# Token pairs innermost in the one-hots of a PEER layer, their products moved from GpSimd to VectorE, and an eight-token multiply issued one step later

## The chip, the cores and the metric

The kernel runs on one core of one Trainium2 chip, as one launch. The metric is device microseconds of that core, the median of a few runs. The engines are named as the profile names them: PE is TensorE (PEld its weight loads), DVE is VectorE, ACT is ScalarE, POOL is GpSimd, SP is the engine that issues most of the transfers.

## The reference

The reference is a chain of three transformer blocks on 256 tokens of width 1024. The change lies in the last layer of the third block, a PEER layer: each token picks, for each of 8 heads, 16 of 16,384 experts, and adds up their value rows, weighted.

```
va, ia = lax.top_k(sa, PEER_TOPK)
vb, ib = lax.top_k(sb, PEER_TOPK)
...
eidx = jnp.take_along_axis(cidx, pos, axis=-1)
g = jax.nn.softmax(top, axis=-1).astype(ht.dtype)
u = u_tab[eidx]
v = v_tab[eidx]
a = jax.nn.gelu(jnp.einsum('thkd,td->thk', u, ht))
return jnp.einsum('thk,thkd->td', g * a, v)
```

An expert's number is `ia * 128 + ib`. The kernel does not gather rows. It computes gelu(u h) for all 16,384 experts and all tokens, multiplies each by the weight that the token gives the expert (zero for nearly all), and multiplies the result with the whole table v.

## The kernel before

All large products run on PE as three products of `fp32r` parts: each weight tile of 128x1024 is loaded by SP (`raw`), rounded by ACT to `hi` (line 66), and DVE subtracts to get `lo` (line 67; every second one of the first half of the `peer_u` stream goes to POOL instead). PE then multiplies `hi` by the high part of the activations, `lo` by the high part and `hi` by the low part: 24 matmuls of 256 columns for each weight tile. One such tile with its 24 matmuls is called a step here. The class `Stream` keeps two steps of split weights ahead of PE (`ahead` = 2, three buffers each of `hi` and `lo`).

The PEER layer (`peer`, from line 1352) runs in this order. The `wq` product gives queries; `topk` finds for each token and each head the 16 experts, in the background of the first half of the `peer_u` product (64 steps). It leaves, in bf16 and with the (head, choice) pairs on the partitions, `iat` and `ibt` (first and second index, 128 x 256 tokens) and `gt` (the softmax weight as a sum of three bf16 parts). The product leaves gelu(u h) in `G[0]`, for the first indices 0 to 63, as 128 partitions (second index) by 64 (first index) by 256 tokens in f32. The second 64 steps of `peer_u` do the same for first indices 64 to 127 (`G[1]`). Then 128 steps of `peer_v` multiply G, split by ACT and DVE in `parts` (lines 128 and 124, `zh` and `zl`), with the table v.

The weights of the tokens are brought in by the generator `weigh(half)` (line 1499), which runs in the background: each step of a product calls it once, before that step's weights are split, and it then issues one block of four tokens (two blocks where `t0 % 60` is 0, so 64 blocks in 59 steps). `weigh(0)` runs during the second half of `peer_u` and `weigh(1)` during the first 60 steps of `peer_v`. A block consists of

- `onehots` for the block two ahead: on DVE `e` (256 elements: is the iota equal to the token's first index) and `ob` (512 elements: the same with the second index), on POOL `oa` = `e` times the three parts of `gt` (768 elements). Their pool has three buffers of each;
- on PE, 12 matmuls of 64 columns (line 1513): for each of four tokens and each part of the weight, `ob` of the token as the stationary operand and `oa` as the moving one, into a PSUM bank of eight tokens by 64;
- in every second block, the multiply of eight tokens of G by that bank on DVE (lines 1515 and 1516, 512 elements), right behind the matmuls that fill it.

In the four tokens of a block, before, the innermost index of every one-hot is the expert's index, and the operands that repeat (`iat`, `ibt`, `gt`) have an innermost step of 0:

```
at = lambda x, n: x[:, t0:t0 + 4].unsqueeze(2).to_broadcast([128, 4, n])
self.tt(e, it[:, :, 64 * half:64 * half + 64].to_broadcast([128, 4, 64]), at(iat, 64), OP.is_equal)
```

The order of the instructions on each engine is the order in which the program issues them; there is no scheduler. In each queue the order around a block is thus: one-hots of the block two ahead, matmuls of the block, multiply of G, then the split of the weights two steps ahead (`hi` on ACT, `lo` on DVE), then the step's 24 matmuls on PE.

Of the kernel before, what the change touches and what calls it, by code (L numbers as in the profile page):

```python
# [11 lines left out]
BF = mybir.dt.bfloat16  # L12
# [3 lines left out]
OP = mybir.AluOpType  # L16
# [5 lines left out]
S = 256  # L22
# [64 lines left out]
class Kern:  # L87
# [1264 lines left out]
    def peer(self, out):  # L1352
        nc, tc = self.nc, self.tc
        st = self.ctx
        gp = st.enter_context(tc.tile_pool(name="g0", bufs=1))
        ip = st.enter_context(tc.tile_pool(name="pidx", bufs=1))
        op_ = st.enter_context(tc.tile_pool(name="oneh", bufs=3))
        G = [gp.tile([128, 64, S], FT, name="G0"), None]
        iat = ip.tile([128, S], BF, name="iat")
        ibt = ip.tile([128, S], BF, name="ibt")  # L1360
        gt = ip.tile([128, S, 3], BF, name="gt")
        iob = ip.tile([128, 128], BF, name="iob")
        tk = ExitStack()
        kp = tk.enter_context(tc.tile_pool(name="topk", bufs=1))
        keys = kp.tile([128, 16, 128], FT, name="keys")
# [1 line left out]
        iota = kp.tile([128, 128], FT, name="iota")  # L1367
# [42 lines left out]
            nc.vector.max_index(idx[:, 8:16], vals[:, 8:16], src)  # L1410

        def topk():
            nc.vector.tensor_copy(iob, iota)
            yield
            for og in range(4):
                if og == 3:
# [11 lines left out]
            for j in range(2):  # L1428
                vv = va[j].rearrange("p (h s) k -> p h s k", s=2)
                for (a, n, c, m) in (0, 4, 0, 16), (4, 12, 64, 4):  # L1430
                    self.tt(cand[:, :, c:c + n * m].rearrange("p h (a b) -> p h a b", b=m),
                            vv[:, :, 0, a:a + n].unsqueeze(3).to_broadcast([128, 8, n, m]),
                            vv[:, :, 1, :m].unsqueeze(2).to_broadcast([128, 8, n, m]), OP.add)
                yield
                for h in range(8):
                    top16(top[:, h], pos[:, h], cand[:, h])
                    yield
                nc.vector.tensor_copy(xf, ix[j].rearrange("p (h s) k -> p s k h", s=2))
                pv = pos.rearrange("p h k -> p k h")
                lt, r1, r2, r3 = pk  # L1440

                nc.vector.tensor_scalar(lt, pv, 6, None, op0=OP.logical_shift_right)
                nc.vector.tensor_scalar(r1, pv, 4, None, op0=OP.logical_shift_right)
                nc.vector.tensor_scalar(r2, pv, 2, None, op0=OP.logical_shift_right)
                self.tt(r3, r2, r1, OP.subtract)
                nc.vector.scalar_tensor_tensor(dk, r3, -12.0, lt, op0=OP.add, op1=OP.mult)
                for s in range(2):
                    if s == 0:
                        self.tt(pf, r1, dk, OP.add)
                    else:  # L1450
                        nc.vector.tensor_scalar(r1, pv, 3, None, op0=OP.bitwise_and)
                        nc.vector.tensor_scalar(r2, pv, 12, None, op0=OP.bitwise_and)
                        nc.vector.scalar_tensor_tensor(dk, lt, -1.0, r2, op0=OP.add, op1=OP.mult)
                        self.tt(pf, r1, dk, OP.subtract)
                    self.tt(eq, pf.unsqueeze(2).to_broadcast([128, 16, 16, 8]),
                            jc.unsqueeze(1).to_broadcast([128, 16, 16, 8]), OP.is_equal)
                    yield
                    self.tt(eq, eq, xf[:, s].unsqueeze(1).to_broadcast([128, 16, 16, 8]), OP.mult)
                    yield
                    for n in (8, 4, 2):  # L1460
                        self.tt(eq[:, :, :n], eq[:, :, :n], eq[:, :, n:2 * n], OP.add)
                    self.tt(sel[:, s].rearrange("p (h k) -> p k h", k=16), eq[:, :, 0], eq[:, :, 1], OP.add)
                    yield
                sg = sel[:, 2].rearrange("p (h k) -> p h k", k=16)
                self.tt(sg, top, top[:, :, 0:1].to_broadcast([128, 8, 16]), OP.subtract)
                nc.scalar.activation(sg, sg, AF.Exp)
                nc.vector.tensor_reduce(zz, sg, axis=AX.X, op=OP.add)
                nc.vector.reciprocal(zz, zz)
                self.tt(sg, sg, zz.unsqueeze(2).to_broadcast([128, 8, 16]), OP.mult)
                yield  # L1470
                ps = self.bank()
                for i in range(3):
                    nc.tensor.transpose(ps[:, 128 * i:128 * i + 128], sel[:, i], self.ident)
                js = slice(128 * j, 128 * j + 128)
                nc.vector.tensor_copy(iat[:, js], ps[:, 0:128])
                nc.vector.tensor_copy(ibt[:, js], ps[:, 128:256])

                nc.vector.tensor_copy(gr[:, 0], ps[:, 256:384])
                nc.vector.tensor_copy(gt[:, js, 0], gr[:, 0])
                for n in (1, 2):  # L1480
                    self.tt(gr[:, n % 2], gr[:, (n - 1) % 2], gt[:, js, n - 1], OP.subtract)
                    nc.vector.tensor_copy(gt[:, js, n], gr[:, n % 2])
                yield
            next(w0)
            yield

        def onehots(half, t0):
            e = op_.tile([128, 4, 64], BF, name="e")
            oa = op_.tile([128, 4, 3, 64], BF, name="oa")
            ob = op_.tile([128, 4, 128], BF, name="ob")  # L1490
            it = iob.unsqueeze(1)
            at = lambda x, n: x[:, t0:t0 + 4].unsqueeze(2).to_broadcast([128, 4, n])
            self.tt(e, it[:, :, 64 * half:64 * half + 64].to_broadcast([128, 4, 64]), at(iat, 64), OP.is_equal)
            nc.gpsimd.tensor_tensor(oa, e.unsqueeze(2).to_broadcast([128, 4, 3, 64]),  # L1494
                                    gt[:, t0:t0 + 4].unsqueeze(3).to_broadcast([128, 4, 3, 64]), op=OP.mult)
            nc.vector.tensor_tensor(ob, it.to_broadcast([128, 4, 128]), at(ibt, 128), op=OP.is_equal)  # L1496
            return oa, ob

        def weigh(half):

            ahead = [onehots(half, 0), onehots(half, 4)]
            yield
            g = G[half]
            for t0 in range(0, S, 4):
                oa, ob = ahead.pop(0)
                if t0 + 8 < S:
                    ahead.append(onehots(half, t0 + 8))
                if t0 % 8 == 0:
                    ps = self.bank()
                for i in range(4):  # L1510
                    c = 64 * (t0 % 8 + i)
                    for n in range(3):
                        nc.tensor.matmul(ps[:, c:c + 64], ob[:, i], oa[:, i, n], start=n == 0, stop=n == 2)  # L1513
                if t0 % 8:
                    gv = g[:, :, t0 - 4:t0 + 4].rearrange("p a t -> p t a")
                    self.tt(gv, ps.rearrange("p (t a) -> p t a", a=64), gv, OP.mult)
                if t0 % 60:
                    yield

        w0 = weigh(0)  # L1520
        self.gemm("wq", 8, [4] * 4, S, self.z_rhs(S), evac_q)
# [317 lines left out]
```

## Time and profile before

| | |
|---|---|
| three runs | 2462.96, 2474.38 and 2479.35 us; median 2474.38 us |
| profiled execution | 2463.75 us, of which the span from first to last instruction is 2462.0 us |
| busy share of the span | PE 96%, DVE 74%, ACT 46%, POOL 13% |
| mean granted clock of PE | 0.974 |
| chain that ended last, by engine | PE 76%, DVE 15%, issue 3%, ACT 2%, DMA 2%, POOL 1% |
| oa on POOL (line 1494) | 128 instructions, 228.7 us |

The shares are means over a long program; only the last quarter of it holds the change. The rows below therefore come from stretches: 1817 to 2037 us is the second half of `peer_u` with `weigh(0)`, 2037 to 2259 us is `peer_v` with `weigh(1)`, and 2259 to 2455 us is `peer_v` without it. Times in rows are us from the start of the span, or ns where the row's head says so. In a timeline row the number after the start is the duration of the instruction; successive starts on one engine are what an instruction costs there, since the end of one overlaps the start of the next a little.

### The profile page before, as it was taken

What the parts mean: (1) busy time and instruction counts of PE and PEld (TensorE: products, weight loads), DVE (VectorE), ACT (ScalarE), POOL (GpSimd) and SP (SyncE); (2) the same over time, 40 slices, a digit from 0 to 9 for tenths busy, and PEclk for the clock granted to TensorE, in tenths of its full rate; (3) what the DMA queues carried; (4) which work ended last, traced back from release to release, by engine and by line L of the source; (5) the groups of instructions that cost most, each with busy time, mean ns of one, the idle gap of its engine ahead of it and who ended that gap; (6) DMA issues with size and microseconds to landing.
All of it is one profiled execution on the core that took longest, in us unless ns stands there. A gap on an engine that the chain in (4) does not pass through costs nothing.

```text
span 2462.0 us, 48311 instructions
## 1 busy us (share of the span) xinstructions
PE 2364.7 (96%) x20162; PEld 2288.8 (93%) x20162; DVE 1834.0 (74%) x2924; ACT 1134.5 (46%) x1509; POOL 315.8 (13%) x180
## 2 busy tenths in 40 slices
PE   8999999999999999998899988999989999999999
PEld 8999879999999979998899987999989998898999
DVE  7777657777767767777965565577989999998554
ACT  5444545444444445444654444444543333333443
POOL 0000000000000000000000000024445544543000
PEclk9999989999999989999899987999999999999999
DMA  6576514575567414676456642455544444444554
GB/s 220 180 238 219 174 47 152 179 233 186 173 204 264 160 53 155 200 245 206 146 190 199 193 139 69 147 177 178 177 146 155 146 159 142 138 139 157 186 188 146
DMA packets 114951, 418.80 MB, mean 170 GB/s; under 512 B 13086, under 2 KB 14382, under 8 KB 113708
## 3 DMA queue, kind: packets, MB, share of 16 engines
q1 hardware_dynamic: 113356, 406.46, 50.3%
q0 software_dynamic: 1376, 9.26, 1.0%
q8 instruction: 157, 2.57, 0.4%
q14 instruction: 62, 0.51, 0.1%
HBM read 414.62 MB, written 1.05 MB: 169 GB/s over the span
## 4 chain that ended last, share of the span: by engine, by line
PE 76%; DVE 15%; issue 3%; ACT 2%; DMA 2%; POOL 1%; SPq 0%; DVEq 0%; ACTq 0%; POOLq 0%
PE b L186 19%; PE b L191 19%; PE b L187 19%; DVE lo L67 5%; PE b L1577 4%; PE b L1575 4%; PE b L1576 4%; DVE G L124 1%; DVE ob L1496 1%; DMA raw<-in_dn 1%; ACT hi L66 1%; PE b L1513 1%; DVE e L124 1%; DVE ut L124 1%; PE b L225 1%
## 5 line engine op out<-in xcount | busy, mean ns | idle before, releaser
L67 DVE TENSOR_TENSOR lo<-raw,hi 128x1024 fp32r<-128x1024 f32 (+1 forms) x690 | 910.9, 1331 | 442.3 <-ACT hi L66 441.5
L66 ACT ACTIVATE hi<-raw 128x1024 fp32r<-128x1024 f32 x722 | 755.4, 1056 | 852.0 <-PE b L191 418.9
L186 PE MATMUL b<-zh,hi 128*128 128x256 f32 (+1 forms) x3504 | 1000.9, 286 | 11.1 <-ACT hi L66 8.0
L187 PE MATMUL b<-zh,lo 128*128 128x256 f32 (+1 forms) x3504 | 991.6, 283 | 13.0 <-DVE lo L67 8.9
L191 PE MATMUL b<-zl,hi 128*128 128x256 f32 (+1 forms) x3504 | 985.9, 283 | 4.4 <-DVE zl L286 3.9
L186 PEld LDWEIGHTS b<-zh,hi 128*128 128x128 f32 x3504 | 664.1, 190 | 19.4 <-ACT hi L66 8.7
L187 PEld LDWEIGHTS b<-zh,lo 128*128 128x128 f32 x3504 | 665.4, 190 | 15.1 <-DVE lo L67 10.0
L191 PEld LDWEIGHTS b<-zl,hi 128*128 128x128 f32 x3504 | 661.9, 190 | 7.2 <-DVE zl L286 7.2
L1577 PE MATMUL b<-zh,lo 128*128 128x256 f32 x1024 | 292.4, 286 | 2.3 <-DVE lo L67 2.3
L1575 PE MATMUL b<-zh,hi 128*128 128x256 f32 x1024 | 294.6, 288 | 0.0
L1576 PE MATMUL b<-zl,hi 128*128 128x256 f32 x1024 | 289.4, 283 | 0.0
L187 PE MATMUL b<-ah,lo 128*128 128x272 f32 (+1 forms) x960 | 270.7, 283 | 4.4 <-DVE lo L67 4.4
L186 PE MATMUL b<-ah,hi 128*128 128x272 f32 (+1 forms) x960 | 270.4, 282 | 0.4 <-ACT hi L66 0.3
L191 PE MATMUL b<-al,hi 128*128 128x272 f32 (+1 forms) x960 | 268.2, 282 | 0.0
L1494 POOL TENSOR_TENSOR oa<-e,gt 128x768 bf16<-128x768 bf16 x128 | 228.7, 1787 | 225.2 <-DVE e L124 195.3
L1577 PEld LDWEIGHTS b<-zh,lo 128*128 128x128 f32 x1024 | 195.2, 191 | 5.8 <-DVE lo L67 4.1
L1576 PEld LDWEIGHTS b<-zl,hi 128*128 128x128 f32 x1024 | 198.3, 194 | 0.0
L1575 PEld LDWEIGHTS b<-zh,hi 128*128 128x128 f32 x1024 | 195.4, 191 | 0.0
L187 PEld LDWEIGHTS b<-ah,lo 128*128 128x128 f32 x960 | 180.6, 188 | 5.4 <-DVE lo L67 5.4
L186 PEld LDWEIGHTS b<-ah,hi 128*128 128x128 f32 x960 | 180.5, 188 | 1.0 <-ACT hi L66 1.0
L191 PEld LDWEIGHTS b<-al,hi 128*128 128x128 f32 x960 | 179.6, 188 | 0.0
L67 POOL TENSOR_TENSOR lo<-raw,hi 128x1024 fp32r<-128x1024 f32 x32 | 79.6, 2489 | 156.9 <-ACT hi L66 147.2
(380 smaller groups left out, 2390.4 us busy)
## 6 DMA issues: line engine op xcount, KB each, us to landing
raw<-in_gu SPq DMA_DIRECT2D x176, 512.0 KB, 4.3
raw<-in_peer_u SPq DMA_DIRECT2D x128, 512.0 KB, 3.3
raw<-in_peer_v SPq DMA_DIRECT2D x128, 512.0 KB, 3.3
raw<-in_dn SPq DMA_DIRECT2D x88, 512.0 KB, 4.6
raw<-in_w_adaT SPq DMA_DIRECT2D x48, 512.0 KB, 4.5
raw<-in_w_up SPq DMA_DIRECT2D x32, 512.0 KB, 4.3
raw<-in_w_down SPq DMA_DIRECT2D x32, 512.0 KB, 4.3
raw<-in_w_in SPq DMA_DIRECT2D x30, 512.0 KB, 4.1
```

The costliest lines, as they stand in the source:

```text
L66: nc.scalar.activation(hi[:, :width], raw, AF.Copy)
L67: (nc.gpsimd if gp else nc.vector).tensor_tensor(lo[:, :width], raw, hi[:, :width].bitcast(FT), op=OP.subtract)
L124: self.nc.vector.tensor_tensor(out, a, b, op=op)
L186: nc.tensor.matmul(outs[o], hi[:, w], xh, start=first, stop=False, skip_group_check=True)
L187: nc.tensor.matmul(outs[o], lo[:, w], xh, start=False, stop=False, skip_group_check=True)
L191: nc.tensor.matmul(out, a, b, start=False, stop=kt == KT - 1, skip_group_check=True)
L225: self.nc.tensor.matmul(ss[:, j:j + 1], sq[:, c:c + 128], self.ones[:, 0:1], start=first and j == 0, stop=last, skip_group_check=True)
L1494: nc.gpsimd.tensor_tensor(oa, e.unsqueeze(2).to_broadcast([128, 4, 3, 64]), gt[:, t0:t0 + 4].unsqueeze(3).to_broadcast([128, 4, 3, 64]), o ...
L1496: nc.vector.tensor_tensor(ob, it.to_broadcast([128, 4, 128]), at(ibt, 128), op=OP.is_equal)
L1575: nc.tensor.matmul(dst, hi[:, w], ah[:, a], start=first, stop=False, skip_group_check=True)
L1576: nc.tensor.matmul(dst, hi[:, w], al[:, a], start=False, stop=False, skip_group_check=True)
L1577: nc.tensor.matmul(dst, lo[:, w], ah[:, a], start=False, stop=last, skip_group_check=True)
```

## The change

The innermost two elements of every one-hot are now two tokens. The four tokens of a block are two pairs; `iob` holds each number twice side by side, and `gt` holds each of its three parts contiguously over the tokens. The products `oa` are three DVE instructions of 256 elements, one for each part, in place of one POOL instruction of 768. On PE the operands of a token are then every second element, for the stationary and the moving operand both. The multiply of G walks eight tokens innermost in G, and is issued at the start of the block after the pair of blocks that filled its bank, behind that block's one-hots.

```
-        gt = ip.tile([128, S, 3], BF, name="gt")
-        iob = ip.tile([128, 128], BF, name="iob")
+        gt = ip.tile([128, 3, S], BF, name="gt")
+        iob = ip.tile([128, 128, 2], BF, name="iob")
...
-            nc.vector.tensor_copy(iob, iota)
+            nc.vector.tensor_copy(iob, iota.unsqueeze(2).to_broadcast([128, 128, 2]))
...
         def onehots(half, t0):
-            e = op_.tile([128, 4, 64], BF, name="e")
-            oa = op_.tile([128, 4, 3, 64], BF, name="oa")
-            ob = op_.tile([128, 4, 128], BF, name="ob")
...
-            self.tt(e, it[:, :, 64 * half:64 * half + 64].to_broadcast([128, 4, 64]), at(iat, 64), OP.is_equal)
-            nc.gpsimd.tensor_tensor(oa, e.unsqueeze(2).to_broadcast([128, 4, 3, 64]),
-                                    gt[:, t0:t0 + 4].unsqueeze(3).to_broadcast([128, 4, 3, 64]), op=OP.mult)
-            nc.vector.tensor_tensor(ob, it.to_broadcast([128, 4, 128]), at(ibt, 128), op=OP.is_equal)
+            e = op_.tile([128, 2, 64, 2], BF, name="e")
+            oa = op_.tile([128, 3, 2, 64, 2], BF, name="oa")
+            ob = op_.tile([128, 2, 128, 2], BF, name="ob")
+            pr = lambda x: x[:, t0:t0 + 4].rearrange("p (q t) -> p q t", t=2)
+            wide = lambda x, n: x.unsqueeze(2).to_broadcast([128, 2, n, 2])
+            two = lambda x: x.unsqueeze(1).to_broadcast([128, 2, x.shape[1], 2])
+            self.tt(e, two(iob[:, 64 * half:64 * half + 64]), wide(pr(iat), 64), OP.is_equal)
+            for n in range(3):
+                self.tt(oa[:, n], e, wide(pr(gt[:, n]), 64), OP.mult)
+            self.tt(ob, two(iob), wide(pr(ibt), 128), OP.is_equal)
             return oa, ob
...
+            def times():
+                ps, t0 = done
+                gv = g[:, :, t0:t0 + 8]
+                self.tt(gv, ps.rearrange("p (t a) -> p a t", a=64), gv, OP.mult)
...
                 if t0 % 8 == 0:
+                    if done is not None:
+                        times()
                     ps = self.bank()
...
-                        nc.tensor.matmul(ps[:, c:c + 64], ob[:, i], oa[:, i, n], start=n == 0, stop=n == 2)
+                        nc.tensor.matmul(ps[:, c:c + 64], ob[:, i // 2, :, i % 2], oa[:, n, i // 2, :, i % 2], start=n == 0, stop=n == 2)
                 if t0 % 8:
-                    gv = g[:, :, t0 - 4:t0 + 4].rearrange("p a t -> p t a")
-                    self.tt(gv, ps.rearrange("p (t a) -> p t a", a=64), gv, OP.mult)
+                    done = ps, t0 - 4
                 if t0 % 60:
                     yield
+            times()
+            yield
```

On DVE, two blocks of `weigh(0)` with the splits `lo` of the weights between them stand in the kernel before like this:

```order
L1496 TENSOR_TENSOR ob<-iob,ibt 128x512
L124 TENSOR_TENSOR G_17694<-b,G_17694 128x8x64
L67 TENSOR_TENSOR lo<-raw,hi 128x1024
L124 TENSOR_TENSOR e<-iob,iat 128x256
L1496 TENSOR_TENSOR ob<-iob,ibt 128x512
L67 TENSOR_TENSOR lo<-raw,hi 128x1024
L124 TENSOR_TENSOR e<-iob,iat 128x256
L1496 TENSOR_TENSOR ob<-iob,ibt 128x512
L124 TENSOR_TENSOR G_17694<-b,G_17694 128x8x64
L67 TENSOR_TENSOR lo<-raw,hi 128x1024
```

And in the changed kernel, on DVE at the same place:

```order
L124 TENSOR_TENSOR G_17694<-b,G_17694 128x64x8
L67 TENSOR_TENSOR lo<-raw,hi 128x1024
L124 TENSOR_TENSOR e<-iob,iat 128x256
L124 TENSOR_TENSOR oa<-e,gt 128x256 x3
L124 TENSOR_TENSOR ob<-iob,ibt 128x512
L67 TENSOR_TENSOR lo<-raw,hi 128x1024
L124 TENSOR_TENSOR e<-iob,iat 128x256
L124 TENSOR_TENSOR oa<-e,gt 128x256 x3
L124 TENSOR_TENSOR ob<-iob,ibt 128x512
L124 TENSOR_TENSOR G_17694<-b,G_17694 128x64x8
```

Each block has three instructions `oa` more on DVE, between `e` and `ob`; the multiply of G still comes once in two blocks, with the loops over tokens and indices exchanged.

On POOL, the last rows of the kernel before, with the splits of the first half of `peer_u` and the products `oa`:

```order
L67 TENSOR_TENSOR lo<-raw,hi 128x1024 x30
L1494 TENSOR_TENSOR oa<-e,gt 128x768 x2
L67 TENSOR_TENSOR lo<-raw,hi 128x1024 x2
L1494 TENSOR_TENSOR oa<-e,gt 128x768 x126
```

On POOL in the changed kernel, at the same place:

```order
L67 TENSOR_TENSOR lo<-raw,hi 128x1024 x32
```

POOL has nothing left to do behind the first half of `peer_u`; before, two products `oa` stood ahead of its last two splits.

## Rows read from the trace of the kernel before

**Rows 1.** Busy time by stretch: `weigh(0)`, `weigh(1)`, and `peer_v` alone.
```profile
core 0: us, PE busy (x) PEld busy (x) DVE busy (x) ACT busy (x) POOL busy (x), PEclk, DMA share, GB/s
1817.00:2037.00 220.00, 212.58 (x2296) 209.06 (x2293) 214.39 (x223) 86.08 (x97) 114.17 (x64) 0.98 0.46 152
2037.00:2259.00 222.00, 204.13 (x2166) 197.40 (x2165) 222.00 (x230) 76.63 (x75) 110.70 (x62) 0.97 0.43 139
2259.00:2455.00 196.00, 196.00 (x1668) 196.00 (x1666) 103.11 (x87) 86.93 (x84) 0.00 (x0) 1.00 0.55 177
```
**Rows 2.** Timeline of DVE in `weigh(1)`: start us, duration us, line, out<-in.
```profile
2101.71 0.41 DVE L124 TENSOR_TENSOR e<-iob,iat 128x256 bf16<-128x256 bf16 x1
2102.05 0.68 DVE L1496 TENSOR_TENSOR ob<-iob,ibt 128x512 bf16<-128x512 bf16 x1
2102.65 2.49 DVE L67 TENSOR_TENSOR lo<-raw,hi 128x1024 fp32r<-128x1024 f32 x1
2105.06 0.41 DVE L124 TENSOR_TENSOR e<-iob,iat 128x256 bf16<-128x256 bf16 x1
...
2106.00 1.34 DVE L124 TENSOR_TENSOR G<-b,G 128x512 f32<-128x512 f32 x1
2107.23 1.26 DVE L67 TENSOR_TENSOR lo<-raw,hi 128x1024 fp32r<-128x1024 f32 x1
2108.41 1.21 DVE L124 TENSOR_TENSOR zl<-G,zh 128x1024 fp32r<-128x1024 f32 x1
2109.55 0.41 DVE L124 TENSOR_TENSOR e<-iob,iat 128x256 bf16<-128x256 bf16 x1
```
**Rows 3.** Timeline of POOL at the same place.
```profile
2102.27 1.79 POOL L1494 TENSOR_TENSOR oa<-e,gt 128x768 bf16<-128x768 bf16 x1 [1.56 <-DVE e L124]
```
**Rows 4.** Timeline of PE at the start of `weigh(1)`, where nothing was late.
```profile
2044.72 0.52 PE L1513 MATMUL b<-oa,ob 128*128 128x64 bf16 x12
2045.08 0.36 PE L1575 MATMUL b<-zh,hi 128*128 128x256 f32 x1
...
2048.00 0.52 PE L1513 MATMUL b<-oa,ob 128*128 128x64 bf16 x12
```
**Rows 5.** Tile G, its multiply on DVE: duration ns min/median/max, first and last start us.
```profile
L124 DVE TENSOR_TENSOR G<-b,G x64: 1235/1337/1364, 1819.5 to 2259.3; 128x512 f32<-128x512 f32 x64
```
**Rows 6.** Timeline of DVE in topk: two dependent bf16 instructions, then one that waits for neither.
```profile
1735.13 1.23 DVE L124 TENSOR_TENSOR ce<-pf,jc 128x2048 bf16<-128x2048 bf16 x1
1736.39 1.23 DVE L124 TENSOR_TENSOR ce<-ce,xf 128x2048 bf16<-128x2048 bf16 x1
1737.53 1.22 DVE L67 TENSOR_TENSOR lo<-raw,hi 128x1024 fp32r<-128x1024 f32 x1
```
**Rows 7.** Groups by form on DVE, columns busy us, mean ns of one, idle before.
```profile
L124 DVE TENSOR_TENSOR ce<-ce 128x256 bf16<-128x256 bf16 x4 | 1.2, 292 | 0.1
L124 DVE TENSOR_TENSOR ce<-ce 128x512 bf16<-128x512 bf16 x4 | 1.7, 426 | 0.1
L124 DVE TENSOR_TENSOR t<-b,r 128x512 f32<-128x512 f32 x11 | 7.5, 683 | 0.0
L124 DVE TENSOR_TENSOR gr<-gr,gt 128x128 f32<-128x128 f32 x4 | 1.2, 292 | 0.1
```
**Rows 8.** Tile sel, written at a step of 64 bytes: ns min/median/max.
```profile
L124 DVE TENSOR_TENSOR sel<-ce x4: 372/388/2471, 1730.6 to 1791.2; 128x128 f32<-128x128 bf16 x4
```
**Rows 9.** Weight loads of a one-hot and of an f32 tile: ns min/median/max.
```profile
L1513 PEld LDWEIGHTS <-ob x1536: 95/98/133, 1816.7 to 2258.8; 128*128 128x128 bf16 x192
L1577 PEld LDWEIGHTS b<-zh,lo x552: 187/188/188, 2260.2 to 2454.8; 128*128 128x128 f32 x184
```
**Rows 10.** Timelines of POOL and PE at the end of the first half of `peer_u`.
```profile
1799.47 1.85 POOL L1494 TENSOR_TENSOR oa<-e,gt 128x768 bf16<-128x768 bf16 x1 [2.91 <-DVE e L124]
...
1803.49 5.65 POOL L67 TENSOR_TENSOR lo<-raw,hi 128x1024 fp32r<-128x1024 f32 x2
...
1806.87 0.38 PE L187 MATMUL b<-zh,lo 128*128 128x256 f32 x1 [4.09 <-POOL lo L67]
```

More of the change, by code (lines that the diff above doesn't have):

```diff
@@ L1478, in topk @@
                 nc.vector.tensor_copy(gr[:, 0], ps[:, 256:384])
-                nc.vector.tensor_copy(gt[:, js, 0], gr[:, 0])
+                nc.vector.tensor_copy(gt[:, 0, js], gr[:, 0])
                 for n in (1, 2):
-                    self.tt(gr[:, n % 2], gr[:, (n - 1) % 2], gt[:, js, n - 1], OP.subtract)
-                    nc.vector.tensor_copy(gt[:, js, n], gr[:, n % 2])
+                    self.tt(gr[:, n % 2], gr[:, (n - 1) % 2], gt[:, n - 1, js], OP.subtract)
+                    nc.vector.tensor_copy(gt[:, n, js], gr[:, n % 2])
                 yield
@@ L1487, in onehots @@
         def onehots(half, t0):
-            e = op_.tile([128, 4, 64], BF, name="e")
-            oa = op_.tile([128, 4, 3, 64], BF, name="oa")
-            ob = op_.tile([128, 4, 128], BF, name="ob")
-            it = iob.unsqueeze(1)
-            at = lambda x, n: x[:, t0:t0 + 4].unsqueeze(2).to_broadcast([128, 4, n])
-            self.tt(e, it[:, :, 64 * half:64 * half + 64].to_broadcast([128, 4, 64]), at(iat, 64), OP.is_equal)
-            nc.gpsimd.tensor_tensor(oa, e.unsqueeze(2).to_broadcast([128, 4, 3, 64]),
-                                    gt[:, t0:t0 + 4].unsqueeze(3).to_broadcast([128, 4, 3, 64]), op=OP.mult)
-            nc.vector.tensor_tensor(ob, it.to_broadcast([128, 4, 128]), at(ibt, 128), op=OP.is_equal)
+            e = op_.tile([128, 2, 64, 2], BF, name="e")
[8 more added lines that the diff above has]
+            self.tt(ob, two(iob), wide(pr(ibt), 128), OP.is_equal)
             return oa, ob
@@ L1503, in weigh @@
             g = G[half]
+            done = None
+            def times():
+                ps, t0 = done
+                gv = g[:, :, t0:t0 + 8]
+                self.tt(gv, ps.rearrange("p (t a) -> p a t", a=64), gv, OP.mult)
             for t0 in range(0, S, 4):
```

## The prediction

> **What bounds the kernel now.** I read the stretches first, since the shares of the whole program say only that PE leads. In `peer_v` alone PE is busy for all of 196.00 us, DVE for 103.11 [rows 1]: PE sets the pace, with 1668 matmuls, so 24 of them (a step) take 196 / 1668 x 24 = 2.82 us. Under `weigh(1)` it is the other way round: DVE is busy for all of 222 us, PE for 204.13; under `weigh(0)` DVE has 214.39 of 220 us and PE 212.58 [rows 1]. What the change touches is there the bound.
>
> The timeline of DVE shows how its time goes [rows 2]. By successive starts `e` costs 0.34 us, `ob` 0.60, the multiply of G 1.23, `lo` 1.18, `zl` 1.14. But the other `lo` of each two blocks costs 2.41: it starts at 2102.65, and `oa` runs on POOL from 2102.27 to 2104.06 [rows 3]. It ends 1.08 us after `oa` does, little less than it needs alone: it stood still while POOL ran. The `lo` behind G starts when POOL is done and pays nothing.
>
> These prices rebuild the stretches. `weigh(0)` has 64 `e`, 64 `ob`, 32 G and 63 `lo` (together the 223 instructions of [rows 1]): 64 x 0.94 + 32 x 1.24 + 63 x (1.18 + 2.41) / 2 = 213 us, against 214.39. `weigh(1)` has 62, 62, 32, 60 and 14 `zl` (230): 58 + 40 + 108 + 16 = 222 us, against 222.
>
> PE's floor: 12 matmuls of a block and the 24 of its step take 2048.00 - 2044.72 = 3.28 us where nothing was late [rows 4], 0.46 more than 2.82; the group itself ends after 0.36. I take 0.42 us for a block. `weigh(0)` holds 2296 - 768 = 1528 wide matmuls, 63.7 steps: 63.7 x 2.82 + 64 x 0.42 = 206 us. `weigh(1)` holds 1398, 58.3 steps: 164 + 27 = 191 us.
>
> **The change part by part.** *oa leaves POOL.* 128 instructions go. POOL's own time bounds nothing, but with them goes the standing still of every second `lo`: 1.23 us x 31 in each stretch, 38 us of DVE each. `e` no longer waits for POOL either.
>
> *oa on DVE, e and ob in the new layout.* No row has an innermost run of two. The lower bound is two elements a cycle, as the bf16 instructions of topk show, which also read an operand again and again in their middle dimension: 2048 elements in 1.23 us, 512 in 426 ns, 256 in 292 ns [rows 6, 7]. The upper bound is today's rate, 256 in 410 ns and 512 in 680 ns [rows 2]. Where an instruction needs the result of the one before, the start comes 0.03 us behind the end (1735.13 + 1.23 to 1736.39), where not, some 0.08 us ahead of it (1736.39 + 1.23 to 1737.53) [rows 6]. So at two a cycle a block costs e 0.32, three oa of 0.21, ob 0.35: 1.30 us; at one a cycle 0.44 + 3 x 0.34 + 0.60 = 2.06. I take 1.30, since the rows of topk have the same operations and type and an operand that repeats.
>
> [...]
>
> *Multiply of G.* Now both the read and the write of G step by 1 KB at each element: 1337 ns [rows 5], against 683 for 512 elements out of PSUM with plain steps [rows 7]. `sel`, with only its write at a step, takes 388 ns for 128 elements against 292 [rows 7, 8], 0.75 ns for each. After the change G runs in eights, and the PSUM bank is read at a step of 256 bytes, which no row shows. Bounds: 683 ns (the step costs nothing) and 1337 (nothing gained, as the one stream costs what two did). I take one stream's price, half of 654 ns, and round down: 0.75 us by starts, from 0.60 to 1.24.
>
> *Order of the multiply.* It goes behind the one-hots of the next block. Those already wait for PE to be done with the buffers of the block before, so it adds no wait; the bank is held a step longer. Behind it in DVE's queue stands `lo`, which PE needs two steps later, so 6 us hide it. The closing multiply of `weigh(1)` comes in its own step, two steps ahead of the first split of `G[1]`. The casts of topk: nothing.
>
> *PE.* Count and order stay. The moving operand steps by 4 bytes; f32 operands do so today and pass 256 columns in 0.117 us. The stationary one: below two bounds. At best nothing changes: 12 loads and matmuls of a block in 0.36 us, 0.03 each. At worst a load of a stepped bf16 tile goes as an f32 one, 188 ns against 98 [rows 9], and as dense as those run today, 0.117 us for each pair: 12 x (0.117 - 0.03) = 1.05 us a block. I take nothing, since the number of weights and the type stay.
>
> *End of the first half of `peer_u`.* Two `oa` stand ahead of POOL's last two splits, and PE waits 4.09 us for a split there [rows 10]. Without them the first split starts up to 5 us earlier, against about 2 us of new one-hots on DVE, on which nobody waits soon. Between 1 and 6 us gained; I take 4.
>
> *The sum.* DVE in `weigh(0)`: 64 x 1.30 + 32 x 0.75 + 63 x 1.18 = 182 us, below PE's 206: PE becomes the bound, 220 to 206, 14 us less. `weigh(1)`: 62 x 1.30 + 24 + 60 x 1.18 + 16 = 191 us, level with PE's 191. Two level engines with G and `zl` at uneven places lose something in spite of the two steps between them; I add 4: 195 against 222, 27 us less. With 4 at the start: 45 us less than 2463.75, **2419 us** on the profiled execution's own terms. The three runs have their median 10.6 us above that execution, and scatter from 2463 to 2479; I add half: **2424 us**. The case's own range: G at 1.24 makes `weigh(1)` 207 us for DVE and takes 12 us away; G at 0.60 and the start at 6 give some 5 more. With the runs' scatter 2405 to 2442.
>
> **Rivals.** *A, a pair of tokens is one word, and repeating it costs.* `iat`, `ibt` and `gt` are read as the same 4-byte word 64 or 128 times, a step at every word. If a step costs what it does in `sel`, 0.75 ns a word [rows 7, 8], then 4 x 128 + 256 words add 0.58 us to a block: DVE 219 us in `weigh(0)` and 227 in `weigh(1)`. That is -1, +5 and -4: no change, 2464 (2469 as a median). For it: every stepped stream of this trace is slow. Against: `e` reads one element 64 times today at full rate, topk eight elements 16 times. [...]
>
> *B, no pairs at all.* The layout then only moves `oa` to DVE: a block at 2.06, 0.76 more, 49 us in `weigh(0)` and 47 in `weigh(1)`: 231 and 238, +11 +16 -3, 2488 own, 2493 as a median. Against it are topk's rows.
>
> *C, PE slows, the other side.* If the stepped weight tiles load like f32, a block costs PE 0.42 + 1.05: 274 us in `weigh(0)` and 258 in `weigh(1)`, +54 +36 -4, 2550. The point from which it decides: 45 us over 128 blocks, 0.35 us a block, 0.03 us a load; beyond that the kernel is slower. For it: the bf16 tile's load is half the f32 one's, which says that packing matters; against: a load hides behind its neighbour's 64 columns as far as the group's 0.36 us shows.
>
> [...] No row here has a strided tile.
>
> **How the numbers follow.** Forecast 0.66, A 0.13, B 0.09, C 0.08, something else near no change 0.04. A measurement of this kernel tells about 1%, 25 us, from no change. The forecast lies 45 us down, and with a dear G and a small start still some 30; a tenth of it falls within 1%. Faster 0.60, same 0.26 (A, the rest, a tenth of the forecast, a third of B), slower 0.14 (C and the rest of B). The range goes from 2405 to 2478: it takes in the forecast and A, leaves out C and B.
>
> **What would show it.** `oa` near 292 ns and `ob` near 426 on DVE: the pairs run; 375 and 600 would be A, 410 and 680 B. No `lo` at 2.49 in `weigh`. G between 0.68 and 1.05 us. The group of line 1513 (1526 after) at 0.52 us still; 1.5 is C. PE busy over 98% of both stretches, DVE near 83% in `weigh(0)` and under 100% in `weigh(1)`, and POOL's 4.09 us wait gone. If all durations come as said and the stretches stay over 215 us, the bound was not DVE, and my reading of the first group is wrong.

## The result and the profile after

| | before | after |
|---|---|---|
| median | 2468.67 us (4 runs, 2456.08 to 2479.35) | 2400.73 us (4 runs, 2398.26 to 2405.79) |
| profiled execution | 2463.75 us | 2399.61 us (span 2397.8) |
| mean granted clock of PE | 0.974 | 0.983 |

The ratio is 0.973, with a 95% interval of 0.968 to 0.978: faster, by 64 us between the two profiled executions where the prediction said 45. The median lies 4 us below the range that was stated (2405 to 2478).

The page of the kernel after, its busy shares and the chain that ended last, shows where the time stands now:

```profile
PE 2325.5 (97%) x20162; PEld 2256.3 (94%) x20162; DVE 1752.0 (73%) x3308; ACT 1135.2 (47%) x1509; POOL 87.8 (4%) x52
...
PE 85%; DVE 9%; ACT 2%; DMA 2%; issue 2%; SPq 0%; DVEq 0%; ACTq 0%
```

PE's share of the chain rose from 76 to 85%, DVE's fell from 15 to 9%, and POOL is gone from it.

To compare stretches, both traces are cut at the same three instructions: the first matmul of a block, the first matmul of `peer_v`, and the last matmul of a block; the last stretch ends with the start of the last `peer_v` matmul. The columns are those of [rows 1]. First the kernel before, then the one after:

```profile
1816.70:2038.10 221.40, 213.98 (x2331) 210.41 (x2329) 215.79 (x225) 86.76 (x99) 114.30 (x64) 0.98 0.46 151
2038.10:2258.90 220.80, 202.93 (x2142) 196.25 (x2138) 220.80 (x229) 75.99 (x75) 110.70 (x62) 0.97 0.43 140
2258.90:2456.50 197.60, 197.60 (x1684) 197.60 (x1681) 104.71 (x90) 87.03 (x84) 0.00 (x0) 1.00 0.54 176
```

```profile
1808.40:2014.20 205.80, 205.80 (x2330) 203.64 (x2329) 176.52 (x419) 86.78 (x99) 0.00 (x0) 1.00 0.49 167
2014.20:2202.10 187.90, 187.90 (x2143) 185.79 (x2140) 178.69 (x413) 76.10 (x75) 0.00 (x0) 1.00 0.49 164
2202.10:2392.30 190.20, 190.20 (x1685) 190.20 (x1682) 103.62 (x89) 87.17 (x84) 0.00 (x0) 1.00 0.54 180
```

PE is now busy for the whole of every stretch. `weigh(0)` is 15.6 us shorter, `weigh(1)` 32.9, `peer_v` alone 7.4, although no edit touches it, and what lies ahead of the first of them 8.3: together the 64. The second profiles of the two kernels, further down, are 53 us apart: 56 in the same three stretches, and 3 the other way ahead of them. So the 8.3 us are in part luck; the gains in the three stretches are not.

On DVE the instructions of a block, by tile (ns min/median/max), answer to [rows 5] and to the durations of [rows 2]:

```profile
L124 DVE TENSOR_TENSOR e<-iob,iat x127: 282/286/293, 1800.1 to 2196.2; 128x256 bf16<-128x256 bf16 x127
L124 DVE TENSOR_TENSOR oa<-e,gt x384: 283/287/294, 1799.2 to 2197.0; 128x256 bf16<-128x256 bf16 x192
L124 DVE TENSOR_TENSOR ob<-iob,ibt x128: 416/421/426, 1799.8 to 2197.2; 128x512 bf16<-128x512 bf16 x128
L124 DVE TENSOR_TENSOR G<-b,G x64: 683/686/692, 1813.2 to 2204.1; 128x512 f32<-128x512 f32 x64
L67 DVE TENSOR_TENSOR lo<-raw,hi x125: 1215/1223/1623, 1801.4 to 2199.6; 128x1024 fp32r<-128x1024 f32 x125
```

`e` and `oa` take 286 ns, `ob` 421: topk's durations for 256 and 512 elements of bf16 [rows 7]. No `lo` reaches 2.49 us any more (the longest is 1.62). The timeline of DVE in `weigh(1)` gives the price of a block by starts:

```profile
2101.08 0.29 DVE L124 TENSOR_TENSOR e<-iob,iat 128x256 bf16<-128x256 bf16 x1
2101.48 0.69 DVE L124 TENSOR_TENSOR oa<-e,gt 128x256 bf16<-128x256 bf16 x3
2102.09 0.42 DVE L124 TENSOR_TENSOR ob<-iob,ibt 128x512 bf16<-128x512 bf16 x1
2102.42 1.22 DVE L67 TENSOR_TENSOR lo<-raw,hi 128x1024 fp32r<-128x1024 f32 x1
2103.56 0.29 DVE L124 TENSOR_TENSOR e<-iob,iat 128x256 bf16<-128x256 bf16 x1
...
2104.90 0.69 DVE L124 TENSOR_TENSOR G<-b,G 128x512 f32<-128x512 f32 x1
2105.50 0.28 DVE L124 TENSOR_TENSOR e<-iob,iat 128x256 bf16<-128x256 bf16 x1
```

From `e` to `lo` it is 1.34 us (`e` 0.40, three `oa` 0.61, `ob` 0.33); `lo` costs 1.14, and G 0.60. On PE a block stands like this, to be read against [rows 4]; the tile's weight loads are below it:

```profile
2100.99 0.54 PE L1526 MATMUL b<-oa,ob 128*128 128x64 bf16 x12
2101.36 0.36 PE L1589 MATMUL b<-zh,hi 128*128 128x256 f32 x1
2101.57 0.28 PE L1590 MATMUL b<-zl,hi 128*128 128x256 f32 x1
```

```profile
L1526 PEld LDWEIGHTS <-ob x1536: 96/98/101, 1808.4 to 2202.1; 128*128 128x128 bf16 x192
```

The next product starts 0.37 us behind the block's first matmul, before it was 0.36 [rows 4]; a load takes 98 ns as in [rows 9]. Operands at a step of two elements cost PE nothing that can be seen. The first wide matmul behind a block is 0.20 us ahead of the next one, in both kernels, where the others are some 0.115 apart; with that a block costs PE 0.46 us.

### The profile page after: what moved, and what is told of

Read it like the earlier page. It is cut to its first block, busy times and chain, and to the rows that moved or that the text cites. A ratio compares the mean times of both kernels' runs of the same rounds, so it can differ in the third digit from the quotient of the medians.

```text
span 2397.8 us, 48499 instructions
## 1 busy us (share of the span) xinstructions
PE 2325.5 (97%) x20162; PEld 2256.3 (94%) x20162; DVE 1752.0 (73%) x3308; ACT 1135.2 (47%) x1509; POOL 87.8 (4%) x52
## 4 chain that ended last, share of the span: by engine, by line
PE 85%; DVE 9%; ACT 2%; DMA 2%; issue 2%; SPq 0%; DVEq 0%; ACTq 0%
PE b L186 21%; PE b L191 21%; PE b L187 21%; PE b L1589 5%; PE b L1590 5%; PE b L1591 5%; DVE lo L67 2%; PE b L1526 2%; DMA raw<-in_dn 1%; ACT hi L66 1%; DVE ut L124 1%; DVE ce L124 1%; PE b L225 1%; PE b L508 1%; DVE zl L286 1%
## 5 line engine op out<-in xcount | busy, mean ns | idle before, releaser
L67 DVE TENSOR_TENSOR lo<-raw,hi 128x1024 fp32r<-128x1024 f32 (+1 forms) x690 | 836.6, 1223 | 452.1 <-ACT hi L66 450.1
L191 PEld LDWEIGHTS b<-zl,hi 128*128 128x128 f32 x3504 | 657.8, 189 | 7.6 <-DVE zl L286 7.6
L1589 PE MATMUL b<-zh,hi 128*128 128x256 f32 x1024 | 288.4, 282 | 0.0
L1590 PE MATMUL b<-zl,hi 128*128 128x256 f32 x1024 | 283.2, 277 | 0.0
L1591 PE MATMUL b<-zh,lo 128*128 128x256 f32 x1024 | 283.0, 276 | 0.0
L1590 PEld LDWEIGHTS b<-zl,hi 128*128 128x128 f32 x1024 | 192.6, 188 | 0.0
L124 DVE TENSOR_TENSOR oa<-e,gt 128x256 bf16<-128x256 bf16 x384 | 89.2, 288 | 13.0
```

The lines of the kernel that those rows point to most:

```text
L67: (nc.gpsimd if gp else nc.vector).tensor_tensor(lo[:, :width], raw, hi[:, :width].bitcast(FT), op=OP.subtract)
L124: self.nc.vector.tensor_tensor(out, a, b, op=op)
L191: nc.tensor.matmul(out, a, b, start=False, stop=kt == KT - 1, skip_group_check=True)
L1589: nc.tensor.matmul(dst, hi[:, w], ah[:, a], start=first, stop=False, skip_group_check=True)
L1590: nc.tensor.matmul(dst, hi[:, w], al[:, a], start=False, stop=False, skip_group_check=True)
L1591: nc.tensor.matmul(dst, lo[:, w], ah[:, a], start=False, stop=last, skip_group_check=True)
```

## The experiments

The theory: in `weigh` DVE was the bound, most of all because `lo` stood still while POOL ran; with `oa` in pairs on DVE this goes, and PE becomes the bound. Rivals: a part of the change would do it alone (moving `oa`, or the walk of G), or the order of the multiply matters. Pairs alone, with `oa` on POOL and G strided, were not run. What was open at first sight is why the stretch behind `weigh(1)`, which no edit touches, became 7.4 us shorter. The stages of all runs, by the cuts above, in us; each ratio stands against the runs of the kernel before that were taken along with it. Bumps are extra matmuls, explained below:

| run | `weigh(0)` | `weigh(1)` | `peer_v` alone | median | ratio, 95% interval |
|---|---|---|---|---|---|
| before | 221.4 | 220.8 | 197.6 | 2468.67 | |
| after | 205.8 | 187.9 | 190.2 | 2400.73 | 0.973, 0.968 to 0.978 |
| oa on POOL | 206.8 | 198.1 | 190.2 | 2419.77 | 0.983, 0.980 to 0.986 |
| old layout, oa on DVE | 241.5 | 240.5 | 190.8 | 2497.98 | 1.013, 1.009 to 1.016 |
| before, G in eights | 221.3 | 220.9 | 197.6 | 2463.61 | 1.000, 0.997 to 1.003 |
| after, G strided | 205.8 | 201.0 | 190.2 | 2412.44 | 0.982, 0.976 to 0.987 |
| after, G in its own step | 205.8 | 187.9 | 190.1 | 2408.80 | 0.977, 0.971 to 0.984 |
| 8 matmuls in a block | 202.6 | 184.5 | 197.7 | 2417.62 | 0.978, 0.972 to 0.984 |
| before again | 221.5 | 220.7 | 197.7 | 2469.43 | 1.001, 0.996 to 1.007 |
| before, with bumps | 221.4 | 220.8 | 195.2 | 2462.04 (1 run) | |
| after, with bumps | 205.8 | 187.9 | 194.5 | 2409.87 (1 run) | |
| 9 matmuls | 204.0 | 185.8 | 197.6 | 2407.26 | 0.980, 0.975 to 0.984 |
| 10 matmuls | 206.8 | 188.0 | 197.6 | 2411.80 | 0.980, 0.975 to 0.984 |
| after again | 205.8 | 187.9 | 190.2 | 2407.70 | 0.978, 0.973 to 0.982 |

The stages of one program repeat to 0.2 us. The medians scatter by more, 2400.73 and 2407.70 for the same kernel: in the profiles of these two the first gelu of `G[0]` stands at 1634.7 and at 1647.4 us, over 170 us ahead of the first block. So what an edit does is read from its stage.

**The products back on POOL, in the new layout.**

```
-                self.tt(oa[:, n], e, wide(pr(gt[:, n]), 64), OP.mult)
+                nc.gpsimd.tensor_tensor(oa[:, n], e, wide(pr(gt[:, n]), 64), op=OP.mult)
```

> The changed kernel with the three products oa of a block back on POOL, in pairs; e, ob and G stay as changed. My theory: DVE was the bound, and each part takes load off it. DVE then has 1.34 - 0.61 = 0.73 us for a block, but every second lo stands still for POOL again, 1.2 us. weigh(1): 62 x 0.73 + 32 x 0.60 + 60 x 1.13 + 14 x 1.13 + 30 x 1.2 = 184 us against PE's 188. So PE stays the bound and the time is that of the changed kernel within 0.5%, 2395 to 2415 us. Rival, that the gain came from freeing POOL and its port: most of it is lost, 2440 us or more.

Measured: `weigh(0)` comes within 1 us of the changed kernel, `weigh(1)` is 10 us longer. The window of `weigh(1)` and the timeline of DVE in it:

```profile
2021.60:2219.70 198.10, 190.27 (x2141) 186.87 (x2137) 198.04 (x227) 75.02 (x73) 178.85 (x186) 1.00 0.46 155
```

```profile
2100.27 0.70 DVE L124 TENSOR_TENSOR e<-iob,iat 128x256 bf16<-128x256 bf16 x1
2100.89 0.41 DVE L124 TENSOR_TENSOR ob<-iob,ibt 128x512 bf16<-128x512 bf16 x1
2101.22 1.63 DVE L67 TENSOR_TENSOR lo<-raw,hi 128x1024 fp32r<-128x1024 f32 x1
```

DVE counts as busy throughout, but `e` takes 0.70 us in place of 0.29 and `lo` 1.63 in place of 1.22: they stand still for POOL, which is busy for 179 of the 198 us. PE's waits in this stretch, 7.8 us, end nearly all with `oa` on POOL (us in total, times, longest):

```profile
PE b L1526 <- POOL oa L1498: 7.6, 11, 1.4
```

The cheaper `e`, `ob` and G, with `oa` in three instructions on POOL, bring 37 of the 48 us that the two stretches lost in the change; the rest needs `oa` off POOL. Neither theory had the size: with `weigh(1)` at PE's floor, 2395 to 2415 was too low. The first theory counted 1.2 us for every second `lo`, where `e` and every `lo` lose some 0.4, and it left out that PE waits for `oa`.

**The products on DVE, everything else as before.**

```
-            nc.gpsimd.tensor_tensor(oa, e.unsqueeze(2).to_broadcast([128, 4, 3, 64]),
+            nc.vector.tensor_tensor(oa, e.unsqueeze(2).to_broadcast([128, 4, 3, 64]),
```

> The kernel before with oa moved to DVE as it stands (one instruction of 768 elements, one innermost token), G as before. My theory: without pairs the one-hots cost DVE 0.34 + 0.03 + 0.87 + 0.60 = 1.84 us a block, and G 1.24: weigh(0) 118 + 40 + 72 = 230 us, weigh(1) 114 + 40 + 68 + 16 = 238 us against 220 and 222; 4 us come back at the end of the first half of peer_u. Slower than before by 15 to 30 us. Rival, that the gain came from freeing POOL and its port: faster than before by 25 us or more.

Measured: 20 us more in each stretch, and slower by 1.3%. The timeline of DVE:

```profile
2104.19 0.42 DVE L124 TENSOR_TENSOR e<-iob,iat 128x256 bf16<-128x256 bf16 x1
2104.71 0.96 DVE L1494 TENSOR_TENSOR oa<-e,gt 128x768 bf16<-128x768 bf16 x1
2105.59 0.68 DVE L1496 TENSOR_TENSOR ob<-iob,ibt 128x512 bf16<-128x512 bf16 x1
2106.19 1.30 DVE L124 TENSOR_TENSOR G<-b,G 128x512 f32<-128x512 f32 x1
```

No `lo` stands still (1.25 us at most), but without pairs the block costs 2.0 us by starts (0.52 + 0.88 + 0.60) against 1.34. PE's waits in the two stretches, 58 us, end with `ob` and `lo` on DVE: with POOL out of the way, DVE's load alone holds PE up. To move the products without the pairs would have been a loss: the pairs are what pays for the move.

**G in eights in the kernel before, nothing else.**

```
-                    gv = g[:, :, t0 - 4:t0 + 4].rearrange("p a t -> p t a")
-                    self.tt(gv, ps.rearrange("p (t a) -> p t a", a=64), gv, OP.mult)
+                    gv = g[:, :, t0 - 4:t0 + 4]
+                    self.tt(gv, ps.rearrange("p (t a) -> p a t", a=64), gv, OP.mult)
```

> The kernel before with only the multiply of G walking eight tokens innermost. G should take 0.69 us in place of 1.34. My theory: little is won, since G covered part of the time in which POOL runs oa; now the lo behind it also meets oa and stands still for 0.6 us. 32 x (0.64 - 0.6): 0 to 10 us faster in all. Rival, that G alone was the surplus on DVE: 20 us less in each weigh, 30 us or more in all.

Measured: no change at all, though the multiply took 677 ns for 1337. The timelines of DVE and POOL show where the 0.65 us went:

```profile
2101.86 0.68 DVE L1496 TENSOR_TENSOR ob<-iob,ibt 128x512 bf16<-128x512 bf16 x1
2102.46 0.68 DVE L124 TENSOR_TENSOR G<-b,G 128x512 f32<-128x512 f32 x1
2103.07 1.89 DVE L67 TENSOR_TENSOR lo<-raw,hi 128x1024 fp32r<-128x1024 f32 x1
2102.08 1.79 POOL L1494 TENSOR_TENSOR oa<-e,gt 128x768 bf16<-128x768 bf16 x1 [1.56 <-PE b L1577]
```

The `lo` behind G took 1.26 us before [rows 2], since POOL was done by the time it began. Now it begins at 2103.07, while `oa` runs until 2103.87, and stands still for the time that G gave back, 1.89 in place of 1.26. The shorter instruction only lengthened the standing still of the next one.

**G strided again in the changed kernel.**

```
-                gv = g[:, :, t0:t0 + 8]
-                self.tt(gv, ps.rearrange("p (t a) -> p a t", a=64), gv, OP.mult)
+                gv = g[:, :, t0:t0 + 8].rearrange("p a t -> p t a")
+                self.tt(gv, ps.rearrange("p (t a) -> p t a", a=64), gv, OP.mult)
```

> The changed kernel with only the multiply of G walking as before (1 KB steps in SBUF), at its new place. G back to 1.34 us. My theory: DVE in weigh(0) 177 + 20 = 197 us stays under PE's 206, no loss; in weigh(1) 186 + 20 = 206 us passes PE's 188, so 15 to 20 us slower than the changed kernel, 2415 to 2422 us. Rival, that G does not matter: same as the changed kernel. On PE's pace: in peer_v alone the wide matmuls went at 117.8 ns in the profile of before and at 113.3 ns in that of after, in stretches that no edit touches. If the change made the pace, this kernel, which is the changed one but for G, has 113.3; if it falls by execution, any kernel shows either.

Measured: `weigh(0)` the same 205.8 us, `weigh(1)` 13.1 longer. The windows of the two:

```profile
1806.60:2012.40 205.80, 205.80 (x2331) 203.66 (x2329) 193.49 (x419) 86.91 (x99) 0.00 (x0) 1.00 0.49 165
2012.40:2213.40 201.00, 191.26 (x2139) 186.77 (x2136) 194.63 (x411) 75.98 (x75) 0.00 (x0) 1.00 0.45 150
```

In `weigh(0)` DVE has 17 us more work and PE covers all of it: 193.49 of 205.80. In `weigh(1)`, where `zl` comes on top and the stretch is shorter, DVE becomes the bound again. The same edit is worth nothing in one stretch and 13 us in the next: with `oa` in pairs on DVE the walk of G pays, alone it does not.

**G multiplied in its own step.**

```
-                    if done is not None:
-                        times()
+                    times()
```

> The changed kernel with the multiply of G issued right behind the matmuls that fill its bank, as before, still eight tokens innermost. My theory: G then waits for a block that PE reaches only after the step before, so DVE, which runs ahead of PE by up to two steps, is held back to PE's place once in two blocks and idles; in weigh(0) it has the slack (177 of 206 us), in weigh(1) hardly (186 of 188). 0 to 10 us slower than the changed kernel. Rival, that the later place is what let PE run without a gap: 20 us or more slower.

Measured: 205.8 and 187.9 us, to the tenth those of the changed kernel. That the multiply comes a step later is worth nothing here; PE is busy throughout in either order.

**Eight narrow matmuls in place of twelve.**

```
-            for n in range(3):
+            for n in range(2):
...
-                    for n in range(3):
+                    for n in range(2):
```

> The changed kernel with the third part of the weights left out: two products oa and 8 matmuls of 64 columns a block in place of three and 12. This leaves out a part of the computation (the lowest 8 bits of each weight's three bf16 parts). My theory: PE is now the bound in both weigh stretches, so the 4 matmuls at 0.03 us come off the time: 128 x 0.12 = 15 us, 2385 us. Rival, that DVE still bounds weigh(1): there 62 x 0.20 = 12 us come off, and 8 in weigh(0), 20 us. Rival, that neither is the bound: no change.

The edit leaves out one of the three `oa` on DVE as well, and with them the lowest bits of the weights.

Measured: 3.2 and 3.4 us off the two stretches, where 64 blocks with four matmuls fewer, at 0.03 us each, should give 7.7 each; and `peer_v` alone, the same instructions, takes 197.7 us, as in the kernel before, where the changed kernel takes 190.2. Neither theory allowed for this. The rows of one 50 us window in that stretch, first the changed kernel, then this one:

```profile
2280.00:2330.00 50.00, 50.00 (x444) 50.00 (x443) 27.37 (x23) 22.92 (x22) 0.00 (x0) 1.00 0.58 195
```

```profile
2280.00:2330.00 50.00, 50.00 (x427) 50.00 (x426) 27.15 (x23) 23.59 (x23) 0.00 (x0) 1.00 0.58 186
```

PE is fully busy in both at a granted clock of 1.00, but one passes 444 matmuls and the other 427: 113 and 117 ns each by this count, which takes in the matmuls at both edges, and 113.3 and 117.8 by successive starts. So a stream of wide matmuls has two paces. The experiments that follow are about this.

**The kernel before, again.**

> The kernel before once more, for PE's pace. If the two paces of the wide matmuls fall by execution and not by kernel, this one may show 113.3 ns in peer_v alone where the first profile of it showed 117.8, and its times scatter by some 20 us; if the change makes the pace, it shows 117.8 ns again from the wq product on.

Measured: in `peer_v` alone again the slow pace, 197.7 us. At the start of `peer_u`, well ahead of the first block, the pace differs from one execution of the same kernel to the next; first the execution profiled before, then this one:

```profile
1600.00:1650.00 50.00, 50.00 (x428) 50.00 (x428) 39.29 (x146) 25.49 (x30) 12.49 (x6) 1.00 0.53 171
```

```profile
1600.00:1650.00 50.00, 50.00 (x444) 50.00 (x443) 37.78 (x133) 27.11 (x32) 9.59 (x5) 1.00 0.52 170
```

So there the program does not fix the pace, and it makes part of the scatter of the medians; behind `weigh` it came out the same.

**Breaks in the stream.** In each of these two, two extra matmuls are put into `peer_v` alone every sixteen steps; their result is used by nobody.

```
+                if i > 15 and a == 0 and i % 4 == 0:
+                    self.warm(2)
```

> The kernel before with two matmuls of 256 columns in bf16 ahead of every sixteenth step of the last 17 times four steps of peer_v. They change nothing in the result. If the pace is a matter of how loads and matmuls fall in step, which a break in the stream sets anew, peer_v alone shows both 113.3 and 117.8 ns, changing at the breaks; if it is a property of the stretch or of the execution, one of them all along.

Measured on the kernel before: 195.2 us for that stretch in place of 197.6, with eight matmuls more in it. Windows ahead of the first break and behind each:

```profile
2259.00:2275.00 16.00, 16.00 (x138) 16.00 (x138) 9.57 (x9) 6.67 (x7) 0.00 (x0) 1.00 0.64 206
2282.00:2317.00 35.00, 35.00 (x299) 35.00 (x298) 18.73 (x17) 16.30 (x16) 0.00 (x0) 1.00 0.57 188
2327.00:2361.00 34.00, 34.00 (x302) 34.00 (x302) 19.11 (x17) 16.58 (x16) 0.00 (x0) 1.00 0.59 192
2371.00:2407.00 36.00, 36.00 (x308) 36.00 (x307) 19.72 (x17) 16.54 (x16) 0.00 (x0) 1.00 0.56 189
2415.00:2450.00 35.00, 35.00 (x311) 35.00 (x310) 18.85 (x16) 15.09 (x15) 0.00 (x0) 1.00 0.42 140
```

Behind the breaks that is 117, 113, 117 and 113 ns a matmul: the pace can change at a break and holds until the next.

> The changed kernel with the two bf16 matmuls of 256 columns ahead of every sixteenth step of peer_v alone, as in the kernel before with bumps, where the pace changed at three of four. If the pace is set anew by each break in the stream of wide matmuls and then holds, peer_v alone starts at 113.3 ns here and goes to 117.8 at one or more of the breaks, some 2 us lost for each such sixteen steps; if the changed kernel has 113.3 ns for a reason of its own that holds on, it stays there.

Measured on the changed kernel: 194.5 us in place of 190.2, and ahead of the first break and behind the first two:

```profile
2208.30:2224.30 16.00, 16.00 (x144) 16.00 (x142) 9.09 (x8) 6.71 (x7) 0.00 (x0) 1.00 0.55 190
2232.00:2266.00 34.00, 34.00 (x291) 34.00 (x291) 18.19 (x16) 15.56 (x15) 0.00 (x0) 1.00 0.56 187
2276.00:2310.00 34.00, 34.00 (x303) 34.00 (x302) 19.10 (x17) 16.29 (x16) 0.00 (x0) 1.00 0.59 197
```

Behind the two later breaks it is 117 and 113 ns again: from the first break on both kernels have the same sequence. With the same breaks in both kernels the 7.4 us between their untouched stretches shrink to 0.7, and of these 0.6 lie ahead of the first break, where one still has the slow pace and the other the fast one (131 matmuls at 4.5 ns). So the gain there is the pace, and not work, data or transfers.

**Nine and ten narrow matmuls.** The third part of the weight is left out for three tokens of four, then for two.

```
-                    for n in range(3):
+                    parts_n = 3 if i >= 3 else 2
+                    for n in range(parts_n):
```

> The changed kernel with the third part of the weights multiplied in for the last token of a block alone: 9 narrow matmuls in place of 12, which leaves out the lowest bits for three tokens of four; DVE as in the changed kernel. PE's count gives 128 x 3 x 0.03 = 11 us less than the changed kernel. If the pace behind a group depends on how many narrow matmuls it has (12: 114.5 ns on average, 8: 117.7), nine may fall on either side: 2390 us with the fast pace, 2408 with the slow one.

> As the one before with the third part for the last two tokens of a block: 10 narrow matmuls, which leaves out the lowest bits for two tokens of four. By count 128 x 2 x 0.03 = 8 us less than the changed kernel, 2393 us with the fast pace, 2410 with the slow one, in weigh and in peer_v alone behind it.

Measured: both have the slow pace in `peer_v` alone, 197.6 us. Nine matmuls win 1.8 and 2.1 us in the two `weigh` stretches, ten lose 1.0 and 0.1 against twelve, though they have less to do. The saved matmuls are given back by the pace: with eight, nine and ten the wide matmuls in `weigh` are 117.4 to 117.8 ns apart, with twelve 114.3 and 114.5 (means of successive starts, the one behind each block left out).

**The changed kernel, again.**

> The changed kernel once more. If the fast pace behind its groups of 12 is a property of the program, weigh and peer_v alone take 205.8, 187.9 and 190.2 us again to within 1 us, whatever the pace in the stretches ahead; if it falls by execution, one of them is some 4% longer.

Measured: all three stages to the tenth of a microsecond as in the first profile, and a median 7 us higher. No version tried is faster than the changed kernel: nine matmuls, which leave out a part of the computation, come to 2407.26, against 2407.70 for this one taken along with them.

## Why the prediction was right or wrong

**The bound: right.** PE is busy for all of both `weigh` stretches, DVE has 176.52 of 205.8 us (86%; 83% was said) and 178.69 of 187.9. The rebuilt sums hold too: 64 x 1.34 + 32 x 0.60 + 63 x 1.14 = 177 us for `weigh(0)`, measured 176.52. In the kernel before, PE's waits in `weigh(1)`, 17.9 us, ended mostly with `oa`, and POOL's own with `e` on DVE, which was never idle there:

```profile
PE b L1513 <- POOL oa L1494: 15.5, 14, 2.8
POOL oa L1494 <- DVE e L124: 102.1, 56, 3.8
```

**A block on DVE: right.** 1.34 us against 1.30. Rival A, the price of a step for each repeated word, falls: `oa` would have taken 375 ns and took 287, `ob` 600 and took 421 (by its own 0.75 ns a word the prediction should have said 388 and 618). A pair of elements read again 64 or 128 times kept the rate of [rows 7]: 286 ns for `e` and 421 for `ob`, against 292 and 426. No run shows a cycle of VectorE, in which the prediction counts its bounds; the traces show 0.52 ns for each further element with pairs (287 to 421 ns) and 1.04 without (411 to 678). Nor did `e` before run at the full rate, as the case against A has it: it took 411 ns, topk's 256 elements 292. Rival B, no pairs, falls by the same numbers, and the run with the old layout on DVE shows what a block costs without them, 2.0 us where B assumed 2.06.

**The multiply of G: mis-sized.** "One stream's price", 0.75 us, was half of the loss of a layout in which read and write both step by 1 KB in SBUF; the read at 256 bytes in PSUM costs nothing (686 ns, the 683 of a plain one [rows 7]). The lower bound, 0.60, was the true price: 5 us less DVE work in each stretch. It had little effect on the time, since PE was the bound already.

**PE's operands: right.** Rival C falls: 0.37 us a block and 98 ns a load. The strided tile's load takes 98 ns, the packed one's took 98 [rows 9].

**POOL and `lo`: right, and the middle of the story.** 38 us of DVE a stretch were put down to `lo` standing still, and the runs show it from three sides: it is gone without `oa` on POOL (1.22 us), it stays in part where POOL does the new `oa` (1.63), and it grows by what G gives back (1.89). What holds it, the port of POOL that two of the expectations name or something else, no run shows; the runs show its times, 2.49, 1.63 and 1.22 us.

**The order of the multiply: right**, worth nothing either way. **The start: right in kind.** POOL's 4.09 us wait is gone. The stretch from the first gelu of G to the first block took 182.9 us before and 173.7 after. Like against like it is 179.7 and 176.0 in the runs with the bumps, where both have the fast pace, and 182.9 and 177.1 in the first profile before and the second after, where both have mostly the slow one. So 4 to 6 us are the edit, where 4 were said, and the rest is pace and scatter: 173.7 and 176.0 are the same program at the same pace.

**The step that failed: "they take 196 / 1668 x 24 = 2.82 us".** A step's price was read from `peer_v` alone of one execution and taken for a constant of the engine, 117.5 ns a matmul. It is the slower of two paces. After the change `peer_v` alone runs at 113.3 ns, 2.72 us a step, and the wide matmuls in `weigh` at 114.3 and 114.5. Of the 19 us by which the profiled execution is faster than forecast, 7.4 lie in `peer_v` alone, which the prediction held unchanged, 4.3 ahead of the first block (pace and scatter), 5.9 in `weigh(1)` and 1.6 in `weigh(0)`. Of the 5.9, 4 are the loss for uneven places, which did not come: PE did not wait. On PE's floor in `weigh` two errors worked against each other. The pace gives 4.9 and 4.2 us (1536 and 1392 wide matmuls), and the blocks take some 2.5 back in each stretch, since a block costs PE the 0.46 us that [rows 4] gave and not the 0.42 that was taken.

The median misses its forecast by 23 us, 4 more than the profiled execution, because it was put 5 us above that execution and came out 1.1 above. So the direction and the mechanism were right, the range a little too narrow, and its lower end rested on a floor that was not one. That the median fell outside by 4 us is within the scatter: the second median of the changed kernel, 2407.70, lies inside. The gains in the three stretches are not scatter; they came again to 0.1 us.

**What stays open** is why the pace behind `weigh` follows the program. It was fast in all profiles with twelve narrow matmuls in a block and paired `oa` (the changed kernel twice, `oa` on POOL, G strided, G in its own step, and with bumps up to the first of them), and slow with eight, nine and ten, and in the kernel before with its waits on DVE (twice, with G in eights, and with bumps up to the first). The old layout on DVE also waits on DVE, and was fast at the end. That a break can set it anew is shown; what inside PE holds it, and what decides which pace a break leaves behind, was not found.

## What to carry to other kernels

Before a saving is booked, ask what stands behind it in its queue: G at half its time brought nothing while the next instruction stood still beside another engine's, and 13 us in one stretch once that was gone. Parts of a change can each be worth nothing or less alone (the walk of G 0, the products on VectorE without pairs 40 us more in the two stretches) and still gain beside the rest, here the pairs. And a floor taken from one stretch of one execution is a sample: look for the same stream elsewhere in the trace, as its pace may differ by 4%.

## What the runs showed of the hardware beyond that

- A stream of 256-column f32 matmuls, each with its weight load, runs at 113.3 or at 117.8 ns a matmul by successive starts, both at a granted clock of 1.00 and both with PE wholly busy. The pace holds for hundreds of matmuls (before and after, for all of `peer_v` alone, some 1680), can change at a break (117 and 113 ns in turn behind those of the bumps), and differs between executions in stretches that no edit touches (428 and 444 in the same 50 us of the kernel before). The busy column can't show it; the count of matmuls in a window does.
- Before, where PE waited 7.4 us in `weigh(0)` and 17.9 in `weigh(1)`, the mean granted clock was 0.98 and 0.97; after, without a wait, it was 1.00 in both. A wait did not always go with a lower clock: in `weigh(1)` with `oa` on POOL and with G strided PE waited 7.8 and 9.7 us at a clock of 1.00. Since DVE was busy for all of `weigh(1)` before, the lower clock was not what bound it there.
- A bf16 operand whose innermost run is two elements, repeated at a step of 0, passed VectorE at the rate of topk's bf16 rows (287 ns for 256 elements, 421 for 512, so 0.52 ns for each further element; 292 and 426 in [rows 7]); one element repeated passed at half of that (411 and 678 ns for 256 and 512, so 1.04 ns; 0.96 us for 768).
- Reading PSUM at a step of 256 bytes cost VectorE nothing (686 ns for 512 f32 elements, 683 for a plain read [rows 7]), while reading and writing SBUF at a step of 1 KB doubled the time (1337 ns).
